# A decoder layer whose instructions are issued from a written list: the list made anew

## The chip, the cores and the metric

The kernel runs on one core of one Trainium2 chip. The metric is the time of one execution on the device, in microseconds (us). A core has a matrix engine (TensorE, PE in the profile), a vector engine (VectorE, DVE), a scalar engine (ScalarE, ACT), a general one (GpSimd, POOL) and a sequencer for transfers (SyncE, SP). Each runs its own instructions strictly in its own order and waits on the others by semaphores.

## The reference

One layer of a hybrid decoder on x of 512 tokens by 1024 features, float32, in this order:

```python
h = h + 0.5 * swiglu(rmsnorm(h, ffn1_norm), w_gate, w_up, w_down)       # FFN1, d_ff = 2816
n = rmsnorm(h, mix_norm)
u, v, z, xbc, dt = split(n @ w_in)
ya = rmsnorm(chunked_spatial_gating(gelu(u), gelu(v), ...))             # causal, chunks of 128
yb = mamba2_mixer(z, xbc, dt, ...)                                      # conv, SSD in chunks of 128
h = h + concatenate([ya, yb]) @ w_out
h = h + 0.5 * swiglu(rmsnorm(h, ffn2_norm), ...)                        # FFN2, as FFN1
h = h + sigmoid(rmsnorm(h, ple_norm) @ ple_w_gate + ple_b_gate) * (p @ ple_w_proj)
return rmsnorm(h, final_norm)
```

swiglu(x) is (silu(x @ w_gate) * (x @ w_up)) @ w_down. All the large products are products of the 512 tokens with weights that are read from HBM once.

## The kernel before

**Products.** Activations lie with features on the partitions. Each float32 operand is split in two parts of a shorter format, a high part and a remainder, and a product is three passes: high by high, high by remainder, remainder by high (`passes`, line 544; `block_product`, line 836). The large products are further done by a scheme of Strassen's kind: for a 2 by 2 block of weights, seven products of sums of blocks instead of eight (`Group.run`, line 880, for gate and up; `down`, line 971, for the way down; `Quads.run`, line 1312, for w_u, w_v and w_z).

**One weight.** A unit of weight is 128 by 1024 float32, 512 KB (`Parts`, lines 490 to 519):

```python
self.raw = sb(self.tag, (P, 1024))
nc.sync.dma_start(self.raw[:, :n], src)                                       # load, issued by SP
nc.gpsimd.dma_start(self.raw[:, : self.n], src, accum_op=ALU.add)             # more, issued by POOL
nc.scalar.copy(self.hi[:, :n], self.raw[:, :n])                               # split: the cast, on ACT
subtract(self.lo[:, :n], self.raw[:, :n], self.hi[:, :n].bitcast(F32))        # the remainder, on DVE
```

A plain weight is one load. Where the scheme wants the sum of two blocks of weights, the second comes in by a transfer that adds to what lies there (`more`); it is issued by POOL, and only when the load of the first has landed. Then follow the cast on ACT (tile `whi`), the subtraction on DVE (`wlo`) and 24 matmuls on PE of 128 by 256. There are three buffers each of `whi` and `wlo`, six PSUM buffers `b` and two `a` (`BANKS`, line 43). An `a` buffer is often begun with a copy, by ACT, of what a `b` buffer holds, and the products are then added on top of it; such a copy is called a seed here.

**The order.** Nothing is issued while the program is first gone through: a `Recorder` notes every operation (line 252). `_units` (line 278) makes 2,925 numbered units of them; successive matmuls into one PSUM tile are one unit, every other operation is one by itself. The string `ORDER` (from line 84) lists all units. At the end, the kernel issues them in that order:

```python
with tc.manual_schedule(engines=ENGINES):
    for u in order:
        for i in units[u]:
            issue(i)
```

The list fixes two things. Each engine runs its own units in the order of the list, and is free to run ahead of or behind the other engines as far as the semaphores let it; the place of a unit in the whole list is not a time. And the buffers are given out in the order of the list: the SBUF places ("rooms", `Rooms.take`, line 369) that have been free longest go first. So the list also says which earlier unit a load must wait for, namely the last user of the room that it gets. All instructions are recorded by the one line of `issue`, so that all have the line L1760 in the profile, and a unit is recognised by its tile and operation.

The units that the prediction names:

| units | what they are |
|---|---|
| 575; 573, 563 | a product of FFN1's gate and up; the cast of its weight, and the copy (seed) that it is added to |
| 581; 578, 579 | the product after it; the load and the cast of its weight |
| 593 | the load of a weight that is used later |
| 643, 648, 653, 669 | loads for the way down of FFN1 |
| 644, 649, 654, 670 | the accumulating transfers on top of these four, in this order |
| 576 | an accumulating transfer for a later product of gate and up |
| 1660, 1661, 1666, 1699 | a subtraction on DVE, the last reader of a weight before 1661 adds to it; three accumulating transfers for w_u |
| 1647, 1693, 1700, 1724, 1832, 1836, 2120 | loads for w_u, w_out and, the last, FFN2 |
| 342; 318 | a product of FFN1; the accumulating transfer for its weight |
| 355, 356 and 435, 436 | loads and the accumulating transfers on top of them, for later products |
| 1835; 1834 | a product of w_out; the subtraction for its weight |
| 1728 | an operation on DVE that reads the PSUM buffer which 1835 takes over |
| 1768 | four small matmuls of the convolution |

Of the kernel before, what the change touches and what calls it, by code (L numbers as in the profile page):

```python
# [73 lines left out]
for _name, _w in _VECS:  # L74
# [10 lines left out]
    "3 4 0-2 5 8 6 14 7 12 36 9 10 72 15 35 24 43 71 37 13 38 42 25 22 20 11 44 47 74 21 45 26 76 49 105 39 "  # L85
    "41 62 16 40 106 18 27 111 50 73 48 51 177 75 77 46 215 172 107 53 61 78 79 112 54 136 52 269 149 187 23 "
    "82 33 63 113 65 80 31 95 29 30 28 108 19 55 84 81 56 59 98 83 99 137 226 86 85 115 32 178 66 109 277 "
    "138 69 68 110 188 96 57 58 87 150 116-118 60 151 114 119 64 139 120 140 162 183 152 173 97 121-125 89 "
    "126 220 335 195 101 127-129 34 174 189 132 133 17 130 131 134 135 102 70 147 145 100 146 227 179 175 "
    "176 190 90 88 92 103 180 153 91 191 193 181 67 184 167 165 163 164 166 185 192 168 196 182 249 186 170 "  # L90
    "197 93 204 148 171 94 143 158 194 216 169 141 221 198 205 250 206 211 217 218 228 251 207 160 212 161 "
    "199 159 208 213 229 219 252 398 263 301 230 231 258-261 242 209 270 271 222-224 233 232 254 243 244 234 "
    "255 210 214 344 235 236 225 245-247 264-266 248 237 256 262 278 306 292 267 144 272 279 273 312 320 349 "
    "307 274 285 238 268 276 302 313 286 280 303 281 308 309 200 201 287 275 304 288 314 282 310 321 322 297 "
    "298 257 305 311 299 289 323 315 316 328 283 293 350 329 290 294 317 291 284 319 336 295 202 330 392 406 "
    "399 337 387 239 393 300 351 338 318 478 355 378 388 435 352 324 331 356 527 421 492 203 389 296 325 353 "
    "340 341 345 156 479 390 430 326 354 240 157 346 357 332 358 347 348 359 379 241 253 380 342 360 394 333 "
    "381 395 363 371 142 372 334 362 364 154 373 343 400 391 401 396 365 366 402 374 375 361 383 403 376 377 "
    "155 397 431 407 384 432 408 385 422 367 423 409 414 424 441 436 528 404 442 443 473 602 327 415 433 484 "
    "564 437 405 368 369 485 386 438 416 426 449 464 521 427 417 444 439 445 410 428 565 522 447 450 440 451 "  # L100
    "434 446 457 474 418 475 419 411 339 452 458 465 476 486 448 480 459 370 481 453 469 460 482 470 466 420 "
    "461 471 493 467 483 507 559 550 516 608 494 535 429 477 517 487 495 488 500 382 518 489 501 529 462 491 "
    "496 463 472 497 519 412 523 508 509 502 510 520 560 524 525 530 561 531 503 532 498 543 544 504 536 526 "
    "562 537 669 490 570 612 653 635 571 533 499 511 538 534 551 552 454 545 572 512 648 539 553 555 513 546 "
    "514 547 643 620 593 578 556 548 505 506 413 566 549 567 540 573 574 557 579 558 455 568 563 575 541 569 "
    "603 580 581 649 675 586 670 654 542 634 594 577 587 595 644 576 588 637 658 425 638 613 456 614 609 589 "
    "596 582 610 468 583 598 554 615 599 584 611 590 621 585 591 622 597 604 605 677 600 645 646 623 629 681 "
    "616 592 650 754 762 793 697 624 685 647 651 515 710 601 636 606 617 607 663 722 794 659 639 630 631 652 "
    "755 618 802 640 655 632 664 619 625 656 657 626 627 641 642 660 676 748 852 661 712 714 693 726 686 689 "
    "679 769 628 633 665 687 662 688 756 711 682 770 763 666 716 671 683 678 713 717 672 738 792 776 684 667 "  # L110
    "673 690 750 703 691 680 723 757 668 734 782 730 694 692 752 695 727 696 674 753 724 751 725 999 698 728 "
    "729 718 699 700 731 719 804 761 768 783 732 743 733 735 715 771 736 737 749 720 758 759 739 805 704 795 "
    "764 705 760 775 777 765 740 721 706 772 1518 784 850 766 778 741 773 767 774 785 779 806 780 786 796 "
    "781 787 803 1000 853 797 701 811 788 798 742 812 744 807 789 813 707 817 745 808 875 883 1045 1065 818 "
    "746 819 814 856 860 854 815 895 864 747 799 708 809 810 823 824 820 879 855 851 821 816 846 847 857 825 "
    "826 822 858 832-834 876 828 877 829 827 790 861 842 835-837 840 830 859 878 862 104 884 880 881 843 863 "
    "702 1125 1035 896 1075 882 865 972 838 844 709 866 885 867 831 845 886 800 839 897 898 868 873 874 841 "
    "1085 962 982 887 899 871 872 890 869 900 901 942 848 902 888 891 791 870 801 849 889 894 892 893 929 "
    "903 973 963 905 906 964 907 904 992 931 908 943 1036 993 909-913 974 944 914-917 994-996 928 965 948 "
    "997 998 1001-1003 919 920 925 930 1014 922 923 1046 924 932 921 945 946 1047 975 1004 1037 1005 1006 "  # L120
    "926 927 956 934 1007 1008 1066 947 1325 1048 1067 935 933 957 1009 1132 1562 1095 1010 1011 983 984 "
    "1012 1013 1049 958 1015 1016 936 949 966 967 1038 1039 959 1050 953 1051 1017 1055 1056 985 1018 1021 "
    "1023 960 1052 939 968 976 977 1022 1057 986 1026 987 978 1086 1218 1019 1190 988 1211 1040 1087 1068 "
    "1024 961 1232 1137 1069 1239 1070 989 1041 1042 1053 1043 1516 1105 979 969 970 990 1054 1058 1059 1234 "
    "1076 980 1156 1193 1138 1253 950 1235 981 1139 1194 1088 1233 1120 1060 1077 952 954 1061-1063 938 951 "
    "991 1197 1064 1192 1096 1222 1028 971 1220 1241 937 1089 1213 1090 1097 955 1191 1212 1078 1079 1020 "
    "940 1071 1072 941 1027 1098 1044 1106 1073 1074 1107 1091 1030 1236 1171 1182 1115 1188 1126 1127 1172 "
    "1092 1176 1177 1173 1198 1215 1214 1242 1216 1511 1323 1349 1318 1130 1542 1029 1221 1195 1201 1131 "
    "1108 1116 1141 1324 1189 1183 1128 1025 1117 1119 1118 1121 1243 1237 1123 1254 1133 1174 1122 1240 "
    "1199 1255 1260 1200 1099 1238 1134 1178 1109 1217 1219 1223 1256 1224 1184 1032 1135 1244 1124 1245 "  # L130
    "1129 1142 1143 1185 1179 1175 1202 1261 1157 1136 1196 1180 1203 1181 1158 1145 1140 1159 1186 1144 "
    "1563 1150 1110 1263 1326 1146 1151 1111 918 1187 1327 1100 1257 1411 1147 1152 1328 1264 1262 1517 1330 "
    "1204 1148 1101 1034 1331 1102 1227 1162 1319 1031 1332 1093 1161 1103 1206 1163 1160 1247 1246 1383 "
    "1249 1258 1153 1229 1432 1412 1033 1390 1265 1320 1259 1112 1334 1080 1164 1321 1350 1386 1205 1329 "
    "1266 1351 1335 1413 1322 1081 1208 1336 1337 1248 1207 1166 1094 1404 1269 1113 1154 1271 1251 1082 "
    "1165 1436 1225 1435 1627 1434 1338 1352 1339 1167 1343 1267 1250 1083 1252 1149 1333 1344 1279 1209 "
    "1425 1446 1268 1354 1353 1169 1512 1345 1355 1210 1340 1513 1226 1428 1274 1155 1341 1356 1461 1453 "
    "1523 1524 1427 1514 1104 1391 1525 1557 1564 1114 1628 1346 1084 1275 1433 1228 1270 1515 1543 1375 "
    "1429 1393 1170 1394 1426 1369 1392 1408 1406 1418 1280 1230 1342 1376 1370 1544 1364 1357 1545 1371 "
    "1272 1372 1231 1519 1273 1276 1365 1520 1460 1366 1405 1277 1647 1521 1168 1407 1387 1536 1430 1522 "  # L140
    "1282 1527 1283 1367 1368 1448 1588 1457 1528 1419 1450 1278 1377 1384 1378 1281 1537 1431 1347 1526 "
    "1284 1373 1415 1285 1381 1529 1374 1437 1395 1565 1286 1531 1438 1440 1398 1379 1447 1414 1385 1530 "
    "1388 1532 1358 1380 1287 1382 1288 1348 1400 1441 1416 1439 1454 1397 1455 1289 1566 1449 1456 1290 "
    "1421 1451 1637 1443 1533 1389 1396 1423 1417 1359 1291 1538 1399 1638 1567 1458 1409 1410 1569 1678 "
    "1654 1402 1292 1570 1548 1535 1558 1652 1549 1401 1539 1571 1293 1362 1361 1629 1360 1363 1559 1463 "
    "1547 1442 1444 1420 1550 1459 1452 1294 1422 1589 1568 1560 1462 1295 1403 1296 1465 1297 1424 1298 "
    "1573 1572 1590 1464 1653 1445 1466 1698 1469 1467 1561 1591 1639 1574 1302 1301 1630 1470 1472 1575 "
    "1468 1582 1471 1473 1303 1546 1300 1475 1476 1540 1576 1659 1577 1578 1474 1552 1299 1477 1631 1478 "
    "1304 1632 1640 1583 1305 1541 1660 1584 1579 1655 1641 1534 1642 1656 1594 1580 1657 1648 1551 1634 "
# [1719 lines left out]
```

## Time and profile before

| what | value |
|---|---|
| median of 3 timed runs | 1036.7 us (1036.21, 1036.7, 1037.64) |
| the profiled execution's own time | 1042.44 us |
| span of the profiled execution | 1040.7 us |
| mean granted clock of TensorE | 0.998 |
| PE busy | 1026.4 us, 7,943 matmuls |
| DVE, ACT, POOL busy | 872.9, 618.8, 107.4 us |
| moved by transfers | 202.24 MB, 194 GB/s on average |

The span goes from the first to the last instruction of the one execution that the profiler recorded; that execution's own time is 1.74 us longer, and 5.74 us over the median of the timed ones. A row of a timeline has the start in us from the span's start, the duration, the engine, line, operation, output<-inputs and count, and in square brackets how long the engine was idle before it and what ended that idle time. SPq and POOLq are the instructions by which SP and POOL issue transfers; a row of the view of transfers has the count, the size of each and the median time from issue to landing. A row of windows has start:end, the length, then busy us and count of PE, PEld (the loading of weights into the array), DVE, ACT and POOL, then the granted clock, the busy share of the transfer engines, and GB/s. A row of the chain of waits has start, length and what ran.

### The profile page before, as it was taken

Reading aid. Unit: us, or ns where it says so; the run is one execution under the profiler, and the core shown is the slowest. Engines: PE = TensorE matmul, PEld = TensorE weight load, DVE = VectorE, ACT = ScalarE, POOL = GpSimd, SP = SyncE. Lnnn points to the kernel's source line nnn. Section 1 sums busy time; section 2 is a strip of 40 time slices with the busy share of each in tenths; the row PEclk is TensorE's granted clock in tenths of the full one; section 3 lists DMA queues with packets and bytes.
Section 4 is the critical chain, followed back from the end, with each engine's and each line's share of the span. In section 5 each row is a group of like instructions: output and inputs, shape, how many; then the busy total and the mean of one; then the engine's idle time right before and its main releaser. Section 6 shows DMA issues by size and latency. Waiting matters only on the chain.

```text
span 1040.7 us, 19641 instructions
## 1 busy us (share of the span) xinstructions
PE 1026.4 (99%) x7943; PEld 974.3 (94%) x7943; DVE 872.9 (84%) x1222; ACT 618.8 (59%) x884; POOL 107.4 (10%) x132
## 2 busy tenths in 40 slices
PE   9999999989999999999999999999999999999997
PEld 7899999989999888899999888899999999999987
DVE  7977876879997889999989875978777879999866
ACT  8645555545656547868867544655545546665646
POOL 1201110111010000100100000011102101011000
PEclk9999999999999999999999999999999999999999
DMA  9899896688958435576675355489959789989302
GB/s 340 273 284 247 228 255 180 186 224 242 284 159 209 140 109 173 121 197 168 138 218 142 121 129 158 120 212 271 231 163 264 185 219 249 306 221 204 112 11 82
DMA packets 60843, 202.24 MB, mean 194 GB/s; under 512 B 6864, under 2 KB 7120, under 8 KB 60752
## 3 DMA queue, kind: packets, MB, share of 16 engines
q1 hardware_dynamic: 37152, 128.47, 34.8%
q0 software_dynamic: 17424, 61.87, 32.3%
q10 hardware_dynamic: 6176, 10.65, 3.5%
q8 instruction: 62, 1.02, 0.4%
q14 instruction: 29, 0.24, 0.1%
HBM read 196.70 MB, written 4.26 MB: 193 GB/s over the span
## 4 chain that ended last, share of the span: by engine, by line
PE 73%; issue 2%; DMA 2%; DVE 1%; ACT 0%; POOL 0%; ACTq 0%; POOLq 0%; DVEq 0%
PE b L1760 46%; PE a L1760 26%; DMA raw<-in_w_u 1%; DMA u<-in_gm_w 0%; DVE wlo L1760 0%; DVE bnst L1760 0%; POOL raw L1760 0%; ACT o L1760 0%; DVE u L1760 0%; DVE raw L1760 0%; ACT m L1760 0%; ACTq L1760 0%; ACT u L1760 0%; ACT a L1760 0%; DVE ny L1760 0%
## 5 line engine op out<-in xcount | busy, mean ns | idle before, releaser
L1760 ACT CAST whi<-raw 128x1024 fp32r<-128x1024 f32 (+1 forms) x233 | 243.2, 1047 | 193.0 <-PE b L1760 86.3
L1760 DVE TENSOR_TENSOR wlo<-raw,whi 128x1024 fp32r<-128x1024 f32 (+1 forms) x232 | 280.8, 1218 | 82.8 <-ACT whi L1760 80.8
L1760 PE MATMUL b<-xf,whi 128*128 128x256 f32 x800 | 139.1, 277 | 0.0
L1760 ACT CAST whi<-rawd 128x1024 fp32r<-128x1024 f32 (+1 forms) x84 | 82.2, 980 | 79.8 <-PE b L1760 32.3
L1760 PEld LDWEIGHTS b<-xf,whi 128*128 128x128 f32 x800 | 120.7, 188 | 0.2
L1760 PE MATMUL b<-xf,wlo 128*128 128x256 f32 x400 | 110.7, 277 | 0.0
L1760 DVE TENSOR_TENSOR wlo<-rawd,whi 128x1024 fp32r<-128x1024 f32 (+1 forms) x84 | 94.3, 1131 | 12.7 <-ACT whi L1760 12.3
L1760 POOL DMA_DIRECT2D raw<-in_ffn_gu x63 | 55.0, 1040 | 426.5 <-DVE wlo L1760 293.1
L1760 PE MATMUL b<-fhi,whi 128*128 128x256 f32 x352 | 98.0, 278 | 0.0
L1760 PE MATMUL b<-flo,whi 128*128 128x256 f32 x352 | 98.0, 278 | 0.0
L1760 PE MATMUL b<-fhi,wlo 128*128 128x256 f32 x352 | 98.0, 278 | 0.0
L1760 PE MATMUL b<-xb,whi 128*128 128x256 f32 (+1 forms) x488 | 97.1, 299 | 0.0
L1760 PE MATMUL b<-xa,whi 128*128 128x256 f32 (+1 forms) x488 | 96.9, 298 | 0.0
L1760 PE MATMUL a<-xb,whi 128*128 128x256 f32 (+1 forms) x448 | 85.1, 290 | 0.0
L1760 PE MATMUL a<-xa,whi 128*128 128x256 f32 (+1 forms) x448 | 84.6, 289 | 0.0
L1760 PEld LDWEIGHTS b<-xa,whi 128*128 128x128 f32 x488 | 76.8, 188 | 4.4 <-ACT xf L1760 0.2
L1760 PEld LDWEIGHTS b<-xb,whi 128*128 128x128 f32 x488 | 76.5, 188 | 4.0 <-issue 0.2
L1760 PE MATMUL a<-xf,whi 128*128 128x256 f32 x400 | 71.7, 282 | 6.0 <-ACT a L1760 6.0
L1760 PEld LDWEIGHTS b<-xf,wlo 128*128 128x128 f32 x400 | 75.2, 188 | 0.0
L1760 PE MATMUL a<-fhi,whi 128*128 128x256 f32 x264 | 73.5, 278 | 0.0
L1760 PE MATMUL a<-flo,whi 128*128 128x256 f32 x264 | 73.5, 278 | 0.0
L1760 PE MATMUL a<-fhi,wlo 128*128 128x256 f32 x264 | 73.5, 278 | 0.0
(405 smaller groups left out, 2663.2 us busy)
## 6 DMA issues: line engine op xcount, KB each, us to landing
raw<-in_ffn_gu SPq DMA_DIRECT2D x109, 512.0 KB, 6.6
raw<-in_ffn_gu POOLq DMA_DIRECT2D x63, 512.0 KB, 8.2
rawd<-in_ffn_down SPq DMA_DIRECT2D x48, 512.0 KB, 6.2
rawd<-in_ffn_down POOLq DMA_DIRECT2D x24, 512.0 KB, 9.2
rawd<-in_ffn_down SPq DMA_DIRECT2D x24, 384.0 KB, 5.3
raw<-in_w_out SPq DMA_DIRECT2D x16, 512.0 KB, 5.2
raw<-in_w_in SPq DMA_DIRECT2D x13, 512.0 KB, 4.1
rawd<-in_ffn_down POOLq DMA_DIRECT2D x12, 384.0 KB, 7.9
```

The costliest lines, as they stand in the source:

```text
L1760: getattr(getattr(real, engine), what)(*(real_of(x) for x in args), **{k: real_of(x) for k, x in kw.items()})
```

## The change

Only the string `ORDER` is replaced: the same 2,925 units stand in another order, which a search made that takes the transfers as served by the moment at which they are issued, and no longer by their place in the list. 2,339 units have another place; those at the places from 840 to 1140 or so are as they were. By engine, of TensorE's 403 units 96 stand at another place among the engine's own, of VectorE's 1,220 842, of ScalarE's 919 660, of GpSimd's 125 80, and of SyncE's 258 204. No unit is added or taken out. Since rooms and buffers follow the list, what a load waits for changes too.

The diff is of 260 lines of numbers; its core, the lines in which the units above stand:

```diff
 ORDER = (
...
-    "399 337 387 239 393 300 351 338 318 478 355 378 388 435 352 324 331 356 527 421 492 203 389 296 325 353 "
...
-    "514 547 643 620 593 578 556 548 505 506 413 566 549 567 540 573 574 557 579 558 455 568 563 575 541 569 "
-    "603 580 581 649 675 586 670 654 542 634 594 577 587 595 644 576 588 637 658 425 638 613 456 614 609 589 "
...
-    "1699 1554 1595 1585 1596 1553 1636 1661 1479-1482 1649 1663 1556 1586 1650 1592 1658 1306 1593 1664 "
-    "1662 1679 1651 2120 1724 1832 1597 1665 1483 1693 1555 1680 1315 1601 1599 1700 1605 1587 1581 1598 "
...
+    "238 322 282 288 304 310 435 378 297-299 257 387 311 314 315 305 239 316 328 323 283 289 290 293 350 356 "
+    "329 294 317 319 291 295 330 436 393 399 318 240 351 202 154 203 156 284 352 324 300 353 388 296 241 "
...
+    "561 503 608 550 562 534 526 543 648 643 512 635 544 504 572 513 538 545 644 539 540 499 511 514 762 653 "
+    "551 455 552 555 556 578 546 593 547 505 553 557 566 541 548 549 567 506 579 573 568 580 558 574 542 563 "
+    "675 575 612 669 569 586 670 576 649 581 515 634 603 587 456 577 637 594 595 613 554 614 582 588 596 468 "
...
+    "1642 1632 1657 1585 1595 1480 1661 1593 1648 1633 1481 1482 1634 1483 1636 1554 1649 1832 1836 1596 "
...
+    "1665 1667 1556 1312 1643 1599 1680 1586 1601 1673 1603 1681 1693 1694 1668 1602 1606 1666 1699 1605 "
...
```

The engines' own orders at the places that the prediction speaks of, taken out of the two lists:

| engine, place | before | after |
|---|---|---|
| SP, FFN1 | ... 648, 643, 620, 593, 578, 658 ... | ... 648, 643, 762, 653, 578, 593, 612, 669, 754 ... |
| POOL, FFN1 | 533, 649, 670, 654, 644, 576 | 533, 644, 670, 576, 649, 654 |
| ACT, FFN1 | 573, 579, 455, 563 | 579, 573, 563 |
| POOL, earlier in FFN1 | 275, 350, 399, 393, 318, 356, 479, 361, 436 | 275, 313, 350, 356, 436, 393, 399, 318 |
| POOL, w_u | 1576, 1699, 1661, 1666 | 1576, 1661, 1666, 1699 |
| SP, w_u | 1698, 2120, 1724, 1832, 1693, 1700 | 1724, 1844, 1647, 1832, 1836, 1678, 1698, 1848, 1693 |
| DVE, end of the mixer | 1834, 18 others, 1728 | 1834, 1728 |
| PE, end of the mixer | 1768, 1748, 1773, two others, 1732, 1743, 1835 | 1748, 1773, 1835, 1768 |

248 rows, old and new, of the table ORDER are left out of this document.

## The prediction

> **What bounds the kernel now.** I read the page first, for the busy shares and the transfers.
>
> ```profile
> span 1040.7 us, 19641 instructions
> PE 1026.4 (99%) x7943; PEld 974.3 (94%) x7943; DVE 872.9 (84%) x1222; ACT 618.8 (59%) x884; POOL 107.4 (10%) x132
> L1760 ACT CAST whi<-raw 128x1024 fp32r<-128x1024 f32 (+1 forms) x233 | 243.2, 1047 | 193.0 <-PE b L1760 86.3
> L1760 DVE TENSOR_TENSOR wlo<-raw,whi 128x1024 fp32r<-128x1024 f32 (+1 forms) x232 | 280.8, 1218 | 82.8 <-ACT whi L1760 80.8
> raw<-in_ffn_gu SPq DMA_DIRECT2D x109, 512.0 KB, 6.6
> raw<-in_ffn_gu POOLq DMA_DIRECT2D x63, 512.0 KB, 8.2
> ```
>
> TensorE (PE) is busy all but 14 us of the span, and the change leaves every matmul in. So only PE's idle time, and time in which its matmuls run slowly, can be won. The view of PE's waits has the whole idle time with a cause:
>
> ```profile
> PE a L1760 <- ACT a L1760: 6.0, 2, 4.7
> PE b L1760 <- DVE tmp L1760: 1.7, 1, 1.7
> PE a L1760 <- ACT whi L1760: 0.5, 1, 0.5
> PE a L1760 <- DVE wlo L1760: 0.2, 1, 0.2
> ```
>
> The 1.7 and 0.5 belong to the start (before the first product) and stay. The 6.0 are two waits for a copy on ScalarE (ACT), of 4.7 and 1.3. The windows and the chain of waits show what the longer one does to the pace:
>
> ```profile
> 156.00:208.00 52.00, 52.00 (x462) 52.00 (x461) 39.67 (x45) 26.78 (x33) 4.82 (x6) 1.00 0.68 182
> 208.00:260.00 52.00, 47.30 (x393) 47.10 (x392) 44.19 (x50) 28.44 (x34) 7.30 (x9) 0.97 0.85 233
> ```
>
> ```profile
> 223.38 4.62 PE a L1760 x24
> ...
> 244.96 50.17 PE b L1760 x426
> ...
> 319.86 28.27 PE a L1760 x240
> ...
> 436.38 5.65 PE b L1760 x48
> ...
> 523.32 11.09 DMA raw<-in_w_u
> ...
> 880.32 55.08 PE b L1760 x486
> ```
>
> After the wait a product of 24 matmuls takes 4.62 us; at the pace of the last row (55.08/486 = 113.3 ns a matmul) it takes 2.72. The granted clock is 0.97 in that window and 1.00 before it. Then PE goes on, with no idle time, at 50.17/426 = 28.27/240 = 117.8 ns, still 117.7 at 436, and is back at 113.3 late in the span: 3.8% slower while the granted clock reads 1.00.
>
> **The first wait (218 us), which the change should remove.**
>
> ```profile
> 218.40 0.28 PE L1760 MATMUL b<-xf,wlo 128*128 128x256 f32 x1
> 223.38 0.50 PE L1760 MATMUL a<-xf,whi 128*128 128x256 f32 x2 [4.70 <-ACT a L1760]
> ```
>
> ```profile
> 221.27 1.04 ACT L1760 CAST whi<-raw 128x1024 fp32r<-128x1024 f32 x1 [7.00 <-DMA raw<-in_ffn_gu]
> 222.22 0.62 ACT L1760 ACTIVATE g<-g 128x512 f32<-128x512 f32 x1
> 222.75 0.58 ACT L1760 COPY a<-b 128x512 f32<-128x512 f32 x1
> ```
>
> ```profile
> 207.50 3.50 POOL L1760 DMA_DIRECT2D rawd<-in_ffn_down  x4 [9.61 <-DVE raw L1760]
> ```
>
> ```profile
> 208.97 1.42 SPq L1760 DMA_DIRECT2D raw<-in_ffn_gu  x2
> ```
>
> ```profile
> rawd<-in_ffn_down POOLq DMA_DIRECT2D x1, 512.0 KB, 5.7
> ...
> rawd<-in_ffn_down POOLq DMA_DIRECT2D x3, 512.0 KB, 12.0
> ...
> raw<-in_ffn_gu SPq DMA_DIRECT2D x1, 512.0 KB, 11.6
> ```
>
> PE waits for the copy at 222.75 (unit 563, the seed of product 575). That copy stands on ACT behind the cast at 221.27 (579), and the cast waits 7.00 us for load 578. 578 is the second of SP's pair at 208.97: issued at about 209.6, landed 11.6 later, where the median load takes 6.6. In front of it are the four accumulating transfers that POOL released at 207.50 in one go (649, 670, 654, 644) and load 593. None of the four is wanted before 578. In the list all four stand some 25 to 35 places behind 578, but POOL runs ahead of its place, and so they are issued 2 us earlier.
>
> In the new list SP issues 578 before 593, and POOL's order is 644, 670, 576, 649, 654. 578 inherits the release that 593 had, so it issues at 208.97. 644 needs only load 643, which now stands earlier, and is through by then. 670 needs its own load 669, now issued after 578 and 593; so it, and with it 576, 649 and 654 behind it on POOL, comes only after some 217 us. With nothing of the four in front, I take for 578 a landing at 208.97 plus 4.2 to 6.6 us (an estimate: the 11.6 less two places of the queue at 3.7, worked out below; and the median), so 213.2 to 215.6. Wanted: PE is free at 218.68, and a cast of 1.05 for 579, one of 1.05 for 573 and a subtraction of 1.22 come before it: 215.4. So the wait goes from 4.70 to 0 to 0.2; I take 0. With it goes the half-speed product, 4.62 − 2.72 = 1.90. Nothing else is late behind it: product 581, the next, uses the cast that was waited for, and so gets it sooner. **Gain 6.60.**
>
> A wait of 1.29 (below) did not draw a half-speed product, the one of 4.70 did. The Trainium skill ("TensorE: Matmul & The Clock Gate", "What's actually happening") has the array fall to half its clock after an idle window of about 3.4 us and return after as long a busy one. The trace agrees in kind, with 4.62 us for one product.
>
> **The second wait (537 us).**
>
> ```profile
> 534.50 1.23 DVE L1760 TENSOR_TENSOR raw<-raw,raw 128x1024 f32<-128x1024 f32 x1 [3.43 <-DMA raw<-in_w_u]
> ```
>
> ```profile
> 538.37 0.50 PE L1760 MATMUL a<-xf,whi 128*128 128x256 f32 x2 [1.29 <-ACT a L1760]
> ```
>
> ```profile
> raw<-in_w_u SPq DMA_DIRECT2D x3, 512.0 KB, 10.7
> ...
> raw<-in_w_u POOLq DMA_DIRECT2D x1, 512.0 KB, 11.1
> ```
>
> The same story, smaller. The chain ends in an accumulating transfer (1661), issued at 523.32 and landed 11.1 later, behind 1699 on POOL and the loads 2120, 1724, 1832, 1693, 1700 that SP sent in the same 5 us. In the new list 1661's own release (unit 1660) stays, but 1699 stands after it, 1724 and 1700 are issued long before, 2120 long after, and 1693 later; 1832 stays and 1836 and 1647 join. With the median of 8.2 us for such a transfer 1661 lands at 531.5 instead of 534.4: 2.9 earlier, where 1.29 and the 0.2 that follows it at 544 are needed. At 11.1 again, nothing is won. I take the former. **Gain 1.51.** Together 8.11.
>
> **What is closer in the new list.** Three places. (C) Product 342:
>
> ```profile
> 102.48 0.85 POOL L1760 DMA_DIRECT2D raw<-in_ffn_gu  x1 [6.79 <-DVE wlo L1760]
> 109.81 1.74 POOL L1760 DMA_DIRECT2D raw<-in_ffn_gu  x2 [6.48 <-DMA raw<-in_ffn_gu]
> ```
>
> ```profile
> raw<-in_ffn_gu POOLq DMA_DIRECT2D x1, 512.0 KB, 9.1
> ```
>
> ```profile
> 122.97 0.39 PE L1760 MATMUL a<-xb,whi 128*128 128x256 f32 x2
> ```
>
> Its weight needs the accumulating transfer 318 (at 102.48, landed 9.1 later, 111.6). In the new list 356 and 436, which were issued at 109.81 or later, stand ahead of 318 on POOL. How long does one more in a row take? Of the four at 207.50 the first landed after 5.7 (213.2), the middle one of the other large three, issued 1.75 us later, after 12.0 (221.2), two places on by the queue: 3.7 to 4 us a place. 111.6 + 2×3.7 = 119.0. Wanted: 122.97 − 1.05 − 1.22 = 120.7. A margin of 1.7, so from below nothing (it was early before, too) to, with 4 us a place and one of them late, 0.6; I take 0.3.
>
> (D) Product 1835:
>
> ```profile
> 575.10 0.42 DVE L1760 TENSOR_TENSOR m<-b,rall 128x256 f32<-128x256 f32 x1
> ```
>
> ```profile
> 576.23 0.61 PE L1760 MATMUL b<-u,convin 128*128 128x128 f32 x4
> ...
> 577.04 0.70 PE L1760 MATMUL b<-m,whi 128*128 128x512 f32 x2
> ```
>
> The PSUM buffer that 1835 writes comes free when DVE's operation at 575.10 (1728) ends, 575.52, so 1.5 us before its use. The new list puts mixing products that stood before 1835 behind it (1768), which asks for it at about 576.23, and gives DVE the subtraction 1834 (1.22) just ahead of 1728: 575.52 + 1.22 − 576.23 = 0.5. Ends: 0, where 1834 runs in an earlier gap, and 1.2, the whole subtraction; I take 0.6.
>
> (E) The first 50 us: SP's first loads change places, but of PE's waits above none is for a transfer there; 0. Everything else that moved stands beside PE at a busy share of 84% (DVE), 59% (ACT) and 10% (POOL), and is priced at nothing for that reason; what it costs where the cover fails is what C and D show, half a microsecond each.
>
> **The sum.** 8.11 − 0.3 − 0.6 = 7.2. The profiled execution took 1042.44 us, 1.74 more than its span, and 5.74 more than the median of the timed runs, 1036.7. 1042.44 − 7.2 = 1035.2 there, and 1036.7 − 7.2 = **1029.5** for the timed runs. Its own range is 1027.5 to 1031.5: C and D at nothing, or at their far ends with half of the second wait kept.
>
> The slow pace is not in this sum. From 228 to 348 us it costs 120×3.8% = 4.6, and up to 442, where shapes are mixed, between nothing and 94×3.8% = 3.6; I take half, 6.4 in all. That is about as much as the profiled execution is above the timed ones, so that the timed ones may never have had it. The Trainium skill ("Runtime: NRT & Kernel Launch", "The ~15µs preamble/postamble breakdown") holds that a profile's total stands a kernel-invariant 6.2 us or so over the time reported without one; by that rule the 5.74 here is no sign of a faster pace, and the timed runs hold the waits and the slow pace alike.
>
> **The rivals.**
>
> (1) *The pace returns as well.* It begins right behind the wait at 218 and not at the shorter one; if the wait sets it off and the timed runs have it, it goes too: 1029.5 − 6.4 = 1023.1. Against it: it lasts 200 us after a cause of 5 us, and the clock reads 1.00.
>
> (2) *The timed runs have less of the waits.* The transfers, crowded to a DMA share of 0.85 in that window, may land earlier when no profile is taken. If the first wait is 2 us instead of 4.70, and so without the half-speed product, 6.60 becomes 2.0: 1034.1.
>
> (3) *The transfers only pile up elsewhere*, by the same margins of a microsecond or two that this list has in many places; or the new list's order on POOL doesn't hold 670 back, since 669 lands early. Then a wait like the first comes back and the time stays at 1036 to 1037.
>
> (4) *The other side: product 342 waits.* If 356 and 436 can't issue sooner than before (436's load 435 is late), 318 goes behind them: 109.81 + 0.87 + 9.1 = 119.8, and another 9.1, 128.9. PE then waits 8.2, and a half-speed product follows, 1.9: 1036.7 − 7.5 + 10.1 = **1039.3**. It decides from a wait of 5.6 us on, that is from a landing of 318 after 126.3. Against it: in the new list 435 stands near 355, some 40 places earlier than before.
>
> **Chances.** Forecast 0.45; (1) 0.17; (2) 0.15; (3) 0.12; (4) 0.11. A measurement of this kernel can tell 0.2%, 2.1 us, from no change. Faster than 1034.6: the forecast, (1), and nearly all of (2), 0.75; within, (3) and the rest of (2), 0.14; slower, (4), 0.11. The range that holds 8 in 10 goes from 1023 to 1037: half of (1) and nearly all of (4) are outside.
>
> **What would show it.** In the changed profile: no wait of PE over 1 us near 218, load 578 landed before 215.4, and POOL's transfers 670, 576, 649, 654 issued after 215. No half-speed product, and clock 1.00 in the window from 208 to 260. 1661 landed before 532, no wait at 537. At 123 PE goes on without a wait (318 landed before 120.7), and less than 1.2 at 577. The pace from 228 to 348 tells (1) from the forecast: 113.3 against 117.8. A wait of PE anywhere else that is longer than 1.5 us makes the prediction wrong, and so does a profiled time that falls while the median doesn't.

## The result: slower, with every wait gone

The changed kernel took 1052.5 us (median of five: 1042.0, 1052.31, 1052.5, 1052.86, 1052.99), the kernel before 1036.7 (median of five, 1036.21 to 1038.27). The ratio is 1.013, with a 95% interval from 1.0081 to 1.0178. The prediction was 1029.5 with a range from 1023 to 1037: wrong, and on the wrong side. Here and below, a ratio leaves out single runs of more than 1.5% over the fastest of the same kernel; a median has all runs.

The page of the changed kernel and its view of PE's waits:

```profile
span 1050.8 us, 19621 instructions
PE 1043.8 (99%) x7943; PEld 992.8 (94%) x7943; DVE 873.6 (83%) x1222; ACT 618.0 (59%) x883; POOL 108.3 (10%) x132
```

```profile
PE b L1760 <- DVE tmp L1760: 1.7, 1, 1.7
```

The waits that the change was predicted to remove are removed, all of them. Only the 1.7 us of the start are left; 6.0, 0.5 and 0.2 us are gone. And yet the same 7,943 matmuls keep PE busy for 1043.8 us in place of 1026.4. The windows show where (columns as in the windows of before):

```profile
52.00:104.00 52.00, 52.00 (x444) 52.00 (x443) 36.98 (x44) 26.08 (x33) 8.56 (x10) 1.00 0.90 244
...
156.00:208.00 52.00, 52.00 (x444) 52.00 (x443) 38.02 (x42) 26.54 (x33) 7.77 (x9) 1.00 0.85 221
208.00:260.00 52.00, 52.00 (x444) 52.00 (x443) 47.88 (x54) 30.18 (x35) 6.90 (x8) 1.00 0.90 241
...
728.00:780.00 52.00, 52.00 (x444) 52.00 (x444) 35.43 (x39) 25.74 (x33) 6.53 (x8) 1.00 0.82 212
```

PE is busy for all of each 52 us and gets 444 matmuls done. Before, it was 462 from 156 to 208. Two more windows of before:

```profile
52.00:104.00 52.00, 52.00 (x461) 52.00 (x460) 38.21 (x42) 26.27 (x32) 7.70 (x9) 1.00 0.98 266
...
728.00:780.00 52.00, 52.00 (x461) 52.00 (x461) 37.71 (x40) 25.85 (x32) 5.65 (x7) 1.00 0.76 197
```

The granted clock is 1.00 in every one of them, so it isn't the clock. It is the slow pace of 117.8 ns a matmul that the prediction had seen behind the wait at 218 (the pace is the time from the start of one matmul to the start of the next; a single one takes 0.28 us and overlaps its neighbours). The chain of waits of the changed kernel has it from end to end:

```profile
50.60 5.65 PE b L1760 x48
...
320.55 28.27 PE a L1760 x240
...
887.09 57.24 PE b L1760 x486
```

5.65/48, 28.27/240 and 57.24/486 are 117.7 to 117.8 ns; the same 486 matmuls took 55.08 us before, 113.3 each. Set side by side matmul by matmul, from the starts of all 7,943, the changed execution falls behind by 6.4 us from 45 to 217 us and by 12.0 from 675 to 985. These are some 64 and 113 products that went from 113.3 to 117.8; 24 matmuls of 4.45 ns more make 6.8 and 12.1 us. It gains 6.4 at the first wait, with the half-speed product, and 1.4 at the second. 18.4 − 7.8 = 10.6, of the 10.1 between the two profiled executions (1042.44 and 1052.5); the rest is in pieces of 0.7 and less at the start, between 540 and 675 us and at the end. (Where the expectations below have 98 or 102 products, 10.5 or 10.9 us, they count too few; the sums by matmul are given with the results.) The two medians are 15.8 apart. The other 5.7 are the distance of the profiled execution of before from its own median, to which the end of this text comes back.

Two paces then, each even to 0.1 ns over hundreds of matmuls. What sets them? What happens in the changed kernel where the pace turns, at 45 us, is hardly to be seen. PE and DVE there, by the timeline:

```profile
44.74 0.40 PE L1760 MATMUL b<-xf,whi 128*128 128x256 f32 x2
44.97 0.33 PE L1760 MATMUL b<-xf,wlo 128*128 128x256 f32 x1
45.14 0.40 PE L1760 MATMUL b<-xf,whi 128*128 128x256 f32 x2
45.37 0.28 PE L1760 MATMUL b<-xf,wlo 128*128 128x256 f32 x1
```

```profile
42.44 1.28 DVE L1760 TENSOR_TENSOR xf<-ft,xf 128x512 fp32r<-128x512 f32 x2
43.64 1.22 DVE L1760 TENSOR_TENSOR wlo<-raw,whi 128x1024 fp32r<-128x1024 f32 x1
```

The third matmul of product 181, the first that needs the remainder `wlo`, takes 0.33 us where the next of its kind takes 0.28: it is 51 ns late (its successor starts 164 ns behind it, where 113 was the pace). The subtraction that makes the remainder, unit 180, ended at 44.86, just too late, since the new list puts the operation 91 in front of it on DVE: the weights for this matmul begin to load 55 ns behind its predecessor's start, where a few ns are usual. No view of waits lists a wait of 51 ns. From the next matmul on the pace is 117.8, until the small matmuls of the mixer at 427.

### The profile page after: what moved, and what is told of

It reads as the page before. It is cut to its first block, busy times and chain, and to the rows that moved or that the text cites. A ratio compares the mean times of both kernels' runs of the same rounds, so it can differ in the third digit from the quotient of the medians.

```text
span 1050.8 us, 19621 instructions
## 1 busy us (share of the span) xinstructions
PE 1043.8 (99%) x7943; PEld 992.8 (94%) x7943; DVE 873.6 (83%) x1222; ACT 618.0 (59%) x883; POOL 108.3 (10%) x132
## 4 chain that ended last, share of the span: by engine, by line
PE 99%; DMA 1%; ACT 0%; SPq 0%; issue 0%; ACTq 0%
PE b L1760 62%; PE a L1760 36%; DMA h<-in_x 1%; ACT o L1760 0%; SPq L1760 0%; ACT ssum L1760 0%; ACT hg L1760 0%; ACT whi L1760 0%; ACTq L1760 0%
## 5 line engine op out<-in xcount | busy, mean ns | idle before, releaser
L1760 PE MATMUL b<-xf,whi 128*128 128x256 f32 x800 | 143.3, 281 | 0.0
L1760 PE MATMUL b<-xa,whi 128*128 128x256 f32 (+1 forms) x488 | 99.1, 302 | 0.0
L1760 PEld LDWEIGHTS a<-xa,whi 128*128 128x128 f32 x448 | 70.2, 189 | 2.2
```

Source lines behind the costliest of these rows:

```text
L1760: getattr(getattr(real, engine), what)(*(real_of(x) for x in args), **{k: real_of(x) for k, x in kw.items()})
```

## The experiments

The theory to be tested, called L in what was expected: the pace is a state that PE keeps while it works without a gap, and that a late matmul can switch. The rivals: T, that PE is slowed when it has no idle time; R, that the pace is drawn anew in each execution, whatever the list. The kernels are permutations of the same units, and in their profiles `issue` is line L1755 or L1756. For one with an exchange only the part of the list that changes is shown.

**One unit moved.** The changed list, with 180 ahead of 91.

```diff
-... 189 179 147 88 190 91 180 176 184 ...
+... 189 179 147 88 190 180 91 176 184 ...
```

> The changed list with one unit moved: VectorE's operation 91 goes behind the subtraction 180, which so ends some 0.7 us earlier and no longer makes the third matmul of product 181 come 51 ns late at 45 us. Theory L (the pace is locked by where a matmul last came late): the products from 45 to 428 us go at 113.3 ns a matmul in place of 117.8; 98 products x 24 x 4.45 ns = 10.5 us less, so some 1042 us, or near 1030 if the second half falls into the faster pace as well. Rival T (TensorE without idle time is slowed): still 117.8 throughout, 1052. Rival R (the pace is drawn anew in each execution): any value from 1030 to 1053, no tie to the edit.

Measured: 1043.03 us (median of 6, 1042.4 to 1045.99), where the changed kernel has 1052.5: 9.5 less for one exchange of two operations that both are still done. The timeline of PE at the same place, and two windows:

```profile
45.10 0.40 PE L1755 MATMUL b<-xf,whi 128*128 128x256 f32 x2
45.34 0.28 PE L1755 MATMUL b<-xf,wlo 128*128 128x256 f32 x1
45.45 0.39 PE L1755 MATMUL b<-xf,whi 128*128 128x256 f32 x2
```

```profile
156.00:208.00 52.00, 51.92 (x457) 51.72 (x457) 41.01 (x47) 27.80 (x34) 7.78 (x9) 1.00 0.87 231
728.00:780.00 52.00, 52.00 (x444) 52.00 (x443) 38.80 (x45) 24.66 (x31) 6.96 (x8) 1.00 0.77 212
```

The matmul is on time, and the pace is 113.3 up to the end of FFN1. (The first window has 457 and not 461, for a matmul at 181 came 0.25 us late; the pace did not turn with it.) Matmul by matmul, this execution draws ahead of the changed kernel's evenly from 46 us on, by 10.6 us up to 360, and by nothing behind that. The second half still has 444 to a window. T falls: from 45 to 181 us PE has the same work and no idle time, and goes at 113.3. The changed kernel's own fifth run, 1042.0, is what this kernel takes; that fits an execution in which the 51 ns happened not to be late, though there is no trace of that run.

**The list of before with its first wait mended.** Three accumulating transfers stand behind 576 on POOL.

```diff
-... 580 581 649 675 586 670 654 542 ... 595 644 576 588 ...
+... 580 581 675 586 670 542 ... 595 576 649 654 644 588 ...
```

> The list of before with three of POOL's accumulating transfers (649, 654, 644) moved behind 576, so that load 578 has only 670 in front of it. All theories: the wait of 4.70 us at 218 is gone. Theory L: with no wait nothing switches the pace, so 113.3 ns goes on to 428 us: 1036.7 - 6.6 = 1030, and up to 6 less if the timed runs had the slow pace too. Rival T: the longer TensorE goes without idle time the sooner it is slowed; 117.8 ns from 218 on as before or from earlier, 1030 to 1037.

Measured: 1032.47 us (median of 6, 1031.27 to 1038.32), ratio 0.9939 (0.992 to 0.9958). The wait at 218 is gone, and most of what the prediction's sum had put on it comes true: 4.2 to 5.4 us less, where 6.6 was expected. The pace did not stay, though, in the one execution that was profiled (1038.32, the slowest of the six). Its PE:

```profile
142.06 0.39 PE L1756 MATMUL a<-xb,whi 128*128 128x256 f32 x2
142.29 0.36 PE L1756 MATMUL a<-xb,wlo 128*128 128x256 f32 x1
142.49 0.40 PE L1756 MATMUL a<-xb,whi 128*128 128x256 f32 x2
```

```profile
84.00:136.00 52.00, 52.00 (x461) 52.00 (x460) 39.58 (x47) 27.00 (x35) 8.64 (x10) 1.00 0.92 242
156.00:208.00 52.00, 52.00 (x444) 52.00 (x443) 37.99 (x44) 26.15 (x32) 5.21 (x6) 1.00 0.63 166
```

A matmul that comes 88 ns late (142.49 follows 142.29 by 201 ns) switched it at 142. So a long wait isn't needed, here as at 45 us, and the prediction's rival (1), by which the wait at 218 sets the pace, has the wrong cause.

**Which half does it.** The two lists hold the same units up to place 1,000 (some 345 us), and up to 2,004 (some 675 us), so they can be joined there.

```diff
-order = changed
+order = changed[:1000] + before[1000:]
```

> The first 1,000 places of the changed list, then the list of before. Theory L: 117.8 ns from 45 to 428 us (the 51 ns late matmul is still there), no wait at 218; then as before, 113.3 from some 550 us on: 64 products at the slow pace up to 218 cost 6.9, the wait's 6.6 are won, so about 1036 to 1038. Rival T: slow to the end but for the wait at 537, some 1050.

Measured: ten runs in two groups, 1028.92, 1030.57, 1031.68, and seven from 1040.02 to 1043.77. The profiled one (1041.24) has the late matmul at 45 us and 117.8 from there to 428, and 461 matmuls in the window from 728 to 780. The groups are some 11 us apart, and 98 products at the slow pace cost 10.5: that fits a race of tens of nanoseconds between DVE and PE, lost in seven runs and won in three, but only one of the ten was traced. So rival R is true in part: one list can take either of two times.

```diff
-order = changed
+order = before[:1000] + changed[1000:]
```

> The first 1,000 places of the list of before, then the changed list. Theory L: 113.3 ns up to the wait at 218, 117.8 behind it up to 428, and in the rest what its own start draws: if as in the changed kernel, 117.8 from 570 to 985 (102 products, 10.9 us): 1036.7 - 1.5 + 10.9 = 1046. Rival T: the same or slower, 1046 to 1050. Were the second half at 113.3, the lock would hang on what came before it and not on the second half's list: 1035.

Measured: 1048.86 us (median of 4, 1047.77 to 1053.01), ratio 1.0107 (1.0078 to 1.0135). The wait at 219 us is there:

```profile
PE a L1755 <- ACT a L1755: 2.7, 1, 2.7
```

A half-speed product of 4.61 us follows it, and behind that the pace is 113.3, not the 117.8 that was expected. So the wait does not set the slow pace. A matmul that came 0.29 us late at 289 us switched it. There are 444 matmuls in the window from 728 to 780, so the second half's list has a cause of its own.

**The swap, with the second half of before.**

```diff
-order = swapped
+order = swapped[:1000] + before[1000:]
```

> The first 1,000 places of the changed list with 91 behind 180, then the list of before: no late matmul at 45 us, and the second half whose pace was 113.3 ns with the list of before. Theory L: 113.3 ns from 45 to 428 and from 663 on; the run with the 51 ns late matmul took 1041.0, less 98 x 24 x 4.45 ns = 10.5 gives 1030.5; the spread between 1029 and 1044 that the run without the swap had is gone. Rival R (the pace is drawn anew in each execution): the same two groups as without the swap, about 1030 and 1041.

Measured: 1033.43 us (median of 12), ratio 0.9948 (0.9919 to 0.9976). The group at 1041 has shrunk but is not gone: eight runs lie from 1029.57 to 1034.51, the other four at 1036.6, 1036.94, 1041.33 and 1051.17. On that chip the kernel before itself ranged from 1034.48 to 1050.94. In the profiled run (1032.1) PE waited once for 1.9 us, and the pace turned to 117.8 at 322 us, behind a matmul 0.1 us late. The direction is as expected by L; that other late matmuls can draw the pace had been left out of the expectation.

**What enters the slow pace in the second half.** In the changed kernel's trace the matmuls of 128 by 512, in the products of w_out ahead of it, take uneven 224 to 240 ns up to 623 us, and then fall, inside product 1855, into an even 226.7. No matmul comes late there, so theory L as it stands does not say why. In all seven traces with that, the 256-wide ones behind go at 117.8; in the seven where the 512-wide ones stay uneven (230 to 231 on average), they go at 113.3. The groups by shape from 640 to 660 us, first of the changed kernel, then of before (the last figures but one are how long a single matmul takes, 389 and 392 to 393 ns, with the overlap):

```profile
L1760 PE MATMUL b<-m,whi 128*128 128x512 f32 x59 | 18.3, 389 | 0.0
L1760 PE MATMUL b<-m,wlo 128*128 128x512 f32 x30 | 11.7, 389 | 0.0
```

```profile
L1760 PE MATMUL b<-m,whi 128*128 128x512 f32 x58 | 18.0, 392 | 0.0
L1760 PE MATMUL b<-m,wlo 128*128 128x512 f32 x30 | 11.8, 393 | 0.0
```

What is quick for the one shape comes with what is slow for the other. PE's order in that stretch differs in few places between the lists, one of them 1855 and 1867.

```diff
-... 1855 1882 1883 1856 2048 ... 1884 1867 1891 1914 1885 1932 1868 1906 ...
+... 1867 1882 1883 1868 2048 ... 1884 1855 1891 1914 1885 1932 1856 1906 ...
```

With the exchange a later operation reads h before one of the two products is added to it, so that what the next stage reads lacks that product; all work is done as before.

> The changed list with 91 behind 180, and in the second half TensorE's products 1867 and 1855 exchanged (with the vector operations 1868 and 1856), which is their order in the list of before. In the changed kernel the 512-wide matmuls fall into an even 226.7 ns inside 1855, at 624 us, and the 256-wide ones that follow go at 117.8 to 985 us. Theory L, with the lock entered inside that product by the sequence of TensorE's own instructions: after the exchange it is entered elsewhere or not at all; if not at all, 113.3 ns from 665 on and 1043.0 - 10.9 = 1032. If the lock hangs on something else in the second half, 1043 as before the exchange.

Measured: 1042.11 us (median of 10), no gain. The even stretch is there again, from 615 us on, inside the product that now stands at that place. So it isn't that product, and the exchange told no more. The next two ask for the place instead.

```diff
-order = swapped
+order = swapped[:2004] + before[2004:]
```

> The changed list with 91 behind 180 up to place 2,004 (some 675 us), then the list of before. In five kernels with the changed list from place 1,000 on the 512-wide matmuls went even at 624 us (226.7 ns) and the 256-wide ones behind them at 117.8 to 985; in five with the list of before there, neither. Theory L, with the pace entered at 624 and kept: 117.8 from 665 to 985 although every unit from 675 on stands as before; some 1043. If the changed list's last part makes the pace: 113.3 there, some 1032.

Measured: ten runs in two equal groups, 1032.23 to 1034.36 and 1042.03 to 1044.46. In the profiled one (1032.85) the even 512-wide stretch is there from 612 us, and the 256-wide matmuls go at 117.8 from its end on, though their list is that of before. Then, at 723:

```profile
723.02 0.28 PE L1755 MATMUL b<-xb,wlo 128*128 128x256 f32 x1
723.54 0.50 PE L1755 MATMUL a<-xa,whi 128*128 128x256 f32 x2 [0.23 <-ACT p L1755]
724.31 0.39 PE L1755 MATMUL a<-xa,wlo 128*128 128x256 f32 x1 [0.27 <-DVE wlo L1755]
```

```profile
660.00:712.00 52.00, 52.00 (x445) 51.68 (x445) 41.81 (x59) 28.76 (x38) 7.47 (x9) 1.00 0.81 208
728.00:780.00 52.00, 52.00 (x462) 52.00 (x461) 38.84 (x44) 26.95 (x34) 7.85 (x9) 1.00 0.70 201
```

Two short waits, 0.5 us together, and the pace is 113.3 for the rest. The expectation of 1043 fits the half of the runs at 1042 to 1044, if no such switch came in them; only the one run was traced.

```diff
-order = swapped
+order = swapped[:1000] + before[1000:2004] + changed[2004:]
```

> The complement: 91 behind 180, the first 1,000 places of the changed list, then those of before up to 2,004, then the changed list. Theory L: no even stretch at 624, so 113.3 ns from 660 to 985 although the last part is the changed one; some 1031 to 1033. If the changed list's last part makes the pace: 117.8 there, some 1043.

Measured: 1031.28 us (median of 8, 1029.2 to 1033.41), ratio 0.9927 (0.9897 to 0.9957). No even stretch, and 459 and 461 matmuls in the windows from 676 and 728. So the changed list's last part is not slow by itself: the pace comes from the places from 1,000 to 2,004 (345 to 675 us), by the traces with the even stretch at 612 to 665, and is kept for the 320 us behind it. What in that part of the list brings on the even stretch stays open.

**How late is late.** Two kernels for product 181, with 0.54 us in place of 51 ns in the changed list, and 0.26 in the list of before.

```diff
-... 190 91 180 176 184 181 92 227 ...
+... 190 91 92 180 176 184 181 227 ...
```

> The changed list with VectorE's operation 92 put ahead of the subtraction 180, so that the third matmul of product 181 comes some 0.7 us late in place of 51 ns. Theory L: a late matmul there can switch the pace; whether 0.7 us draws the slow pace as 51 ns did is open: 117.8 ns from 45 us and 1053 if any lateness does it, 113.3 ns and some 1043 if only a lateness of a small size does.

```diff
-... 92 103 180 153 ... 184 167 165 ...
+... 92 103 167 180 153 ... 184 165 ...
```

> The list of before with VectorE's operation 167 put ahead of the subtraction 180, so that the third matmul of product 181 comes some 0.25 us late, where it was not late. Theory L, if any lateness there draws the slow pace: 117.8 ns from 45 us to the wait at 218, 64 products x 24 x 4.45 ns = 6.8 us more, some 1044. If the list of before holds its pace over this lateness, 1037 to 1038.

Measured: 1044.76 us (eight runs, five from 1043.15 to 1044.82, three from 1053.2 to 1053.93) and 1041.89 (eight, 1034.32 to 1055.43). In neither profiled execution did the late matmul at 45 us switch the pace: 461 matmuls in the windows that follow (in the second it turned at 143 us, behind a matmul 77 ns late). So a lateness can go with a switch, and not every lateness does; for the three runs at 1053 there is no trace. I counted, over the fourteen profiled executions, the matmuls that started at least 130 ns after the one before, in stretches of 256-wide ones with a clear pace on both sides. Of 42 at the 113.3 ns pace, 13 were followed by 117.8; of 18 at 117.8, 10 were followed by 113.3. (The same places of the lists recur in several traces, so these are not 60 separate cases.) In the long stretches (45 to 340 us and 680 to 985) the pace never changed without one.

**A wait put in.** If that is so, then a late matmul in the slow second half should make the kernel faster.

```diff
-... 2017 2037 2042 2064 ...
+... 2017 2042 2037 2064 ...
```

> The changed list with 91 behind 180, and one wait put in: VectorE's operation 2042 (1.2 us) stands ahead of the subtraction 2037, which so ends some 0.6 us too late for the third matmul of product 2038 at 689 us (679 with the swap). TensorE is then at the slow pace, and of the six matmuls that came more than 0.25 us late at the slow pace in the traces so far, all six were followed by the fast one. Theory L: the wait costs 0.6 and the 256-wide products behind it, to 985, go at 113.3: 97 x 24 x 4.45 ns = 10.4 less; 1043.0 - 9.8 = 1033. Rival T, or a pace that the list's last part makes: 1043.6.

Measured: 1031.25 us (median of 10, eight of them from 1030.07 to 1031.62), 11.8 less than the kernel without the wait (1043.03, on another chip, on which the kernel before took 1037.84; here it took 1037.77), and ratio 0.9952 (0.9933 to 0.9971) to the kernel before. PE at the place, and the window behind it:

```profile
677.96 0.40 PE L1755 MATMUL b<-xf,whi 128*128 128x256 f32 x2
678.35 0.39 PE L1755 MATMUL b<-xf,wlo 128*128 128x256 f32 x1
678.57 0.40 PE L1755 MATMUL b<-xf,whi 128*128 128x256 f32 x2
678.81 0.28 PE L1755 MATMUL b<-xf,wlo 128*128 128x256 f32 x1
```

```profile
728.00:780.00 52.00, 52.00 (x461) 52.00 (x460) 39.55 (x44) 26.84 (x33) 6.95 (x8) 1.00 0.82 221
```

The matmul at 678.35 comes 0.15 us late (not 0.6; DVE had some time to spare), and 461 are done in a window in place of 444. Matmul by matmul, this execution and that of the kernel without the wait stay together from 575 to 675 us and draw apart evenly from there, by 11.2 us up to 985. A wait of 0.15 us was worth some 11. This is the clearest of the runs: TensorE's own list is as it was, and all that is added for it is a delay. The expectation's six out of six is no rule: in this same trace a matmul that came 0.31 us late at the slow pace, at 530 us, was followed by the slow pace.

**The kernel before once more.**

> The kernel before, unchanged, for a second profile of it. Its timed runs lie between 1034.5 and 1050.9, the one profiled execution took 1042.44. Theory L: the wait at 218 is there in each execution; the pace behind it is not the same in each, 113.3 ns where the time is near 1036 and 117.8 where it is near 1042.

Measured: 1038.16 us for a span of 1036.4. Its view of PE's waits:

```profile
PE a L1760 <- ACT a L1760: 2.5, 1, 2.5
PE b L1760 <- DVE tmp L1760: 1.7, 1, 1.7
PE a L1760 <- ACT whi L1760: 0.7, 1, 0.7
PE b L1760 <- DVE m L1760: 0.5, 1, 0.5
PE a L1760 <- DVE wlo L1760: 0.2, 1, 0.2
```

The wait at 218 is there, but 2.5 long and with no half-speed product behind it; the pace behind it is 117.8 all the same, up to 425. So the profiled execution of before on which the prediction built, 1042.44, was a long one of a kernel that ranged, over the chips used here, from 1033.58 to 1050.94, and the expectation that the pace tells 1036 from 1042 is not borne out. The second wait, at 537 us, is not there at all: the product that had come 1.45 us late comes 0.1 us late here, and no later in the five other traces with the list of before in that stretch.

## Why the prediction was wrong, step by step

**The waits: right in mechanism.** Load 578 was issued first of its pair, POOL's four no longer stood in front of it (644 landed at 212.85, the other three were issued from 223 on), and it landed 4.9 us after its issue where 11.6 had been. The view of transfers of the changed kernel, for the moments of issue of 578, 1661 and 318:

```profile
raw<-in_ffn_gu SPq DMA_DIRECT2D x1, 512.0 KB, 4.9
...
raw<-in_w_u POOLq DMA_DIRECT2D x1, 512.0 KB, 7.4
...
raw<-in_ffn_gu POOLq DMA_DIRECT2D x1, 512.0 KB, 16.6
```

4.9 lies inside the predicted 4.2 to 6.6. 1661 took 7.4 where 8.2 was taken. 318, the place of rival (4), was issued at 105.25 and landed 16.6 later, at 121.8, later than the 119.0 worked out; but PE was 3.8 us later by then, and asked for it at 124.5. That PE was late by the slow pace is not what saved it: in the kernel with 180 ahead of 91, at the fast pace, 318 landed at 120.6 and 342 began at 123.99 without a wait. None at 577 either, where 0.6 had been put. The predicted gain of 8.11 is 7.8 in the two profiled executions. Some of that is luck: the second wait, 1.51 of the 8.11, was in the one profile of before that the prediction had read and in none of the six other traces with that stretch of the list. Two of its sums come out otherwise, without weight for the result: C and D at nothing give 1028.6 and the far ends some 1031.1, where its own range says 1027.5 to 1031.5, and of the two landings, 8 us over two places of the queue, comes 4.0 a place and not 3.7.

**"Only PE's idle time, and time in which its matmuls run slowly, can be won": the step that failed.** The prediction read both paces off the trace and treated the slower one as something that could only go away. It took 113.3 ns for the pace of every stretch that was not disturbed before. But a new list moves the moments at which matmuls come late, and with one of these moments the pace was lost at 45 us; it was lost again in the second half. Nothing in the sum stood for losing it. With the 177 products that lost it, 18.4 us, it was the largest term there was.

**(E), the first 50 us put at 0, and all else "priced at nothing" beside PE, DVE at its busy share of 84%: mis-sized.** The loss in the first half came from here: subtraction 180, 0.6 us later than need be. As a wait it cost 51 ns, and the price of nothing was right to that. What it drew cost 10.6 against the same list without it. The loss of the second half, 12.0, came from the list's places 1,000 to 2,004 (345 to 675 us), where the prediction looked (the second wait, and place D) only for waits. What sets it off there stays open.

**Rival (1)** had the right quantity and the wrong cause: the pace is not the echo of a long wait, which was followed by 113.3 in two traces (before's first half with the changed second, and before with 167 ahead of 180, where it ended a slow stretch) and by 117.8 in the two of before. **Rival (2)** was right as far as the two profiles of before go: in the second the wait is 2.5 and not 4.7, without the half-speed product, and of the 4.3 us between the two executions 3.8 lie between 200 and 300 us. **Rival (4)** was on the right side by a mechanism that didn't happen. The chance of 0.11 for slower was the chance of that mechanism, and not of all that could go wrong with a list in which 2,339 places differ. Nor could 0.2% be told from no change: the interval of the result itself is 0.5% to either side.

**The 5.74 us between the profile and the median.** The prediction left the slow pace out of the sum because of them. It is no constant: each time reported here is its own span plus some 1.7 to 2.1, the kernel before gave 1042.44 and 1038.16 under the same profiler, and both lie in the range of its timed runs. The Trainium skill ("Runtime: NRT & Kernel Launch", "The ~15µs preamble/postamble breakdown") has a kernel-invariant 6.2 us between the total time of a profile and the time that the runtime reports. The 5.74 stood between two executions, so that rule did not bear on it, and no run here shows the 6.2.

With the late matmul at 45 us out of the way and the fast pace in the second half, by the places 1,000 to 2,004 of before or by the added wait, the kernel takes 1031.3, or 6.5 less than the kernel before on the same chip, where 7.2 had been forecast. That the two are near is in part luck: set beside the second profile of before, the kernel with the added wait gains 2.9 us at the first wait and 4.3 by the faster pace behind it, up to 340 us. The version with the changed list's first and last part and the middle of before (ratio 0.9927) and the one with the added wait (0.9952) both beat the two kernels of this case.

## What to carry to other kernels

When the bounding engine is busy without a gap, its pace is a quantity of its own: count its instructions per stretch in both profiles before explaining a difference by waits, and put a term for a change of pace into the sum, with both signs, when the trace shows two. A view of waits doesn't list 50 ns; where a pace turns, look at the starts of single matmuls. And a kernel whose runs fall into groups some 1% apart may have such a switch in it: take traces of both groups before comparing medians.

## What the runs showed of the hardware

A stream of 256-wide matmuls, each with its own load of weights, ran at 113.3 or at 117.8 ns a matmul, at a granted clock of 1.00 both times, and kept either for some 300 us on end. In the count above, a matmul that came late, by 18 ns to 4.9 us, was followed by the other pace in 23 of 60 cases, by the same one in 37. 512-wide matmuls ran at an even 226.7 or an uneven 230 to 231 ns on average, and the even ones were followed by the slower of the two paces of the 256-wide in seven traces of seven. An idle time of TensorE of 2.7, 4.4 and 4.7 us was each followed by one product at half speed (4.6 us), one of 2.5 us was not. The Trainium skill ("TensorE: Matmul & The Clock Gate", "Back-to-back issue gap") gives N/2.4 + 2.5 ns for a single matmul in isolation, from which I estimate 109.2 for 256 and 215.8 for 512, and a measured 131 ns at 512 for a sustained stream. The traces have two paces for each shape, 4 to 15 ns above the first figure, and none near the 131. What in TensorE holds that state, why one lateness switches it and another does not, and what brings on the even stretch with no matmul late, stays open: 51 ns at 45 us went with a switch, 0.54 and 0.26 us at the same place did not in the executions that were profiled.
